# A hybrid encoder step on one core: another order of work inside the attention loop, a lower rate of convolution taps, and fill steps placed elsewhere

## The chip, the cores and the metric

The kernel runs on one core of one Trainium2 chip. A core has five engines that run beside each other, each with its own queue of instructions in order: TensorE (PE in the profile; its weight loads are PEld), VectorE (DVE), ScalarE (ACT), GpSimd (POOL) and SyncE (SP, which here issues DMAs). Matmul results land in PSUM, from which ACT or DVE must copy them out before the buffer can be used again. The metric is the device time of one execution in microseconds (us); less is better.

## What is computed

One layer of a streaming encoder. Its input is 1024 tokens of a new stream and 32 tokens of a running one, each of 1024 channels (1056 tokens in all). What follows is the reference with all that bears on the change:

```
h = rmsnorm(x) ; projections of h: q, k, v, f, ga, ua, ub, gb, ma, mb
q, k = per-head rmsnorm (16 heads of 64) ; c = cumsum(log_sigmoid(f + b_f))
s[t, s'] = q[t].k[s'] + c[t] - c[s']   masked to s' <= t
o = softmax(s) @ v                      # 8 query blocks of 128; block i has (i+1)*128 keys
u = ua * sigmoid(ub)
conv = causal depthwise conv(u), width 31
yb = silu(layernorm(conv) * ln_g + ln_b) * silu(gb) @ w_pb
ya = (o * silu(ga)) @ w_pa
y = x + (sigmoid(ma) * ya + sigmoid(mb) * yb) @ w_out
```

The 32 tokens of the running stream attend to 512 cached keys and to themselves.

## The kernel before

Each of the 1024 columns of a projection group is made in eight weight tiles of 128 columns. Float32 is kept by splitting weights and input into a high and a low half-precision part and adding three products per 128 channels. One weight tile gives three chunks of 352 tokens; one chunk is eight *fill steps* of three matmuls each (`steps`, with `mms` at line 183). After each fill step `beat()` runs: it counts beats and issues whatever is due then, such as parts of the next weight tiles' split (`Batch`: high part on ACT, L138, low part on DVE, L141), and convolution taps, which it hands out at `pace["rate"]` taps a beat.

The convolution runs on DVE: 31 instructions a channel tile (L371), one a tap. When the last channel tile is done, its sum and its sum of squares are added up, and `sides["ready"]` is set; from then on the layernorm's generator (`layernorm`) is advanced by one piece in each step of the attention loop. It first makes the column mean of three chunks with a matmul of ones (L1202), then the variance of three chunks the same way, and then the inverse root in six pieces.

The change is in the attention stage. There PE, SP, DVE and ACT follow the order written in the source (`manual_schedule`); POOL's order is left to the scheduler. `seq` is the list of 132 pieces: 16 heads with eight query blocks each (`Block`, i = 0 to 7), and four pieces of the running stream (`Sample`), each put behind block 0 of heads 3, 7, 11 and 15. The loop takes one piece of `seq` a step and works on several of them at different stages:

- `start`, which is `scores` of piece n+3: the score matmuls on PE into a PSUM tile of tag S (two buffers; L1121, L1122), then on DVE the causal mask added (L1124) and the row maximum (L1126).
- `soft` of piece n+3: the exponential and its row sum on ACT (L1133).
- `norm` of piece n+2: the reciprocal of the row sum on DVE (L1138), and the scaling of the probabilities on POOL (L1139).
- `turn` of piece n, the turning: PE transposes the probabilities in blocks of 128 keys into PSUM tiles of tag T (L1153), up to four blocks in one tile, so blocks i = 4 to 7 need two tiles. The first tile is copied out by ACT, the second by DVE (L1156). POOL zeroes a part of the copy's target (L1146).
- `values` of piece n-2: only at i = 7, for the whole head, 20 products (L1172) into two tiles of tag T, copied and added by ACT (L1176) and DVE (L1177), and multiplied by the gate at odd heads (L1179). At i = 5 of odd heads it only loads that gate. A `Sample` has its own, smaller `values` (L1090).
- `finish` of a `Sample` at piece n-3: one more transpose into tag T (L1099), copied by ACT and DVE.
- `fill(k)`: k fill steps of the 22 gate weight tiles that are kept for this stage (528 fill steps). Their result goes to its own PSUM tiles and is copied out by ACT (L942, L944) and stored by SP.
- the layernorm's piece, whose matmuls (L1202) also use tag T.

Tag T has only two PSUM buffers for all of these: turnings, values, finishes, the layernorm's column sums, and a small sum for each pair of weight tiles (L126).

Of the kernel before, what the change touches and what calls it, by code (L numbers as in the profile page):

```python
# [8 lines left out]
F32 = mybir.dt.float32  # L9
# [5 lines left out]
ALU = mybir.AluOpType  # L15
AX = mybir.AxisListType

D = 1024
T = 1024
# [6 lines left out]
CH = 352  # L26
# [4 lines left out]
LNO = ((0,), (1, 2), (3,), (4, 5), (6,), (7,), ())  # L31
LNEXP = "natural_log_exp_and_others"
NFILL = 22
R_U, R_V, R_QK, R_G, R_A = 0.21, 0.18, 0.165, 0.23, 0.2
NWARM = 34
HT = TT // 2
HC = HT // 2
# [16 lines left out]
def build(tc, xT, xt, wv, wf, ckT, cv, clT, stT, vec, cst, yT, kT, vO, lfO, cpT, csT):  # L54
    nc = tc.nc
# [3 lines left out]
    def pool(name, bufs=1, stack=es, **kw):  # L59
        return stack.enter_context(tc.tile_pool(name=name, bufs=bufs, reuse_waits="tile", **kw))  # L60
# [19 lines left out]
    rstd = lnp.tile([128, TT], F32, name="rstd")  # L80
# [105 lines left out]
    def csl(c):  # L186
        return slice(c * CH, (c + 1) * CH)
# [88 lines left out]
    def t352(name, bufs):  # L276
        return sg.tile([128, CH], F32, name=name, tag=name, bufs=bufs)
# [5 lines left out]
    class Banks:  # L283

        n = 0
# [221 lines left out]
    def newton(out, v, y):  # L507

        nc.vector.tensor_mul(out, y, y)
        nc.vector.scalar_tensor_tensor(out, out, -0.5, v, op0=ALU.mult, op1=ALU.mult)  # L510
        nc.vector.scalar_tensor_tensor(out, out, 1.5, y, op0=ALU.add, op1=ALU.mult)
# [225 lines left out]
    for c in range(4):  # L737
# [16 lines left out]
        for t in range(8):  # L754
            ps = pj.tile([128, 512], F32, name="pjv", tag="pj")
            n = 0
            for kt in range(KT):
                sl = slice(t * 128, t * 128 + 128)
# [243 lines left out]
    psT = pool("psT", 2, stack=p2, space=PS)  # L1002
# [4 lines left out]
    class Two:  # L1007
        n = 0
# [14 lines left out]
    def fill(n):  # L1023
        for _ in range(n):
            next(flow, None)
# [157 lines left out]
    seq = []  # L1183
# [5 lines left out]
    def start(b):  # L1189
        if getattr(b, "i", 1) == 0:  # L1190
            h = b.head
            if h.h % 2 == 0:
                h.ot = heads[h.h + 1].ot = ap.tile([128, T], F32, name="ot", tag="ot", bufs=2)
        b.scores()

    def pending(b):
        return isinstance(b, Sample) or b.i % 2

    def over_channels(acc, put):
        for c in range(3):  # L1200
            pm = psT.tile([128, 512], F32, name="psn", tag="T")
            nc.tensor.matmul(pm[:, :CH], ones_f, acc[:, csl(c)], start=True, stop=True)  # L1202
            put(csl(c), pm[:, :CH])
            yield

    def layernorm():

        shift = sides["shift"]
        for _ in range(4):
            yield  # L1210
        yield from over_channels(mean, lambda sl, ps: nc.scalar.mul(mean[:, sl], ps, 1.0 / D))

        def put(sl, ps):
            t = t352("t", 3)
            nc.scalar.activation(t, mean[:, sl], AF.Square)
            nc.vector.scalar_tensor_tensor(rstd[:, sl], ps, 1.0 / D, t, op0=ALU.mult, op1=ALU.subtract)
            nc.vector.tensor_add(mean[:, sl], mean[:, sl], shift[:, sl])
            nc.vector.tensor_scalar(rstd[:, sl], rstd[:, sl], EPS, None, op0=ALU.add)

        yield from over_channels(rstd, put)  # L1220
        for c in range(6):
            sl = slice(c * CH // 2, c * CH // 2 + CH // 2)
            v, y = rstd[:, sl], t352("t", 3)[:, :CH // 2]
            nc.scalar.activation(y, v, AF.Ln)
            nc.scalar.activation(y, y, AF.Exp, scale=-0.5)
            yield
            w = t352("t", 3)[:, :CH // 2]
            nc.vector.tensor_copy(w, v)
            newton(v, w, y)
            yield  # L1230

    ones_f = cp.tile([128, 128], F32, name="ones_f", tag="ob")
    nc.vector.memset(ones_f, 1.0)
    ln = layernorm()
    sides["shift"] = ap.tile([128, TT], F32, name="shift", bufs=1)
    nc.sync.dma_start(sides["shift"], s_m)
    heads[1].load()
    for n in range(3):
# [3 lines left out]
            seq[n - 1].norm()  # L1242
        fill((8, 4, 0)[n])
    for n, b in enumerate(seq):
        if n + 3 < len(seq):
            start(seq[n + 3])
        if n + 9 < len(seq) and getattr(seq[n + 9], "i", 1) == 0:
            seq[n + 9].head.load()
        if n + 6 < len(seq) and isinstance(seq[n + 6], Sample):
            seq[n + 6].load()  # L1250
        if getattr(b, "i", 0) == 3 and b.head.h + 1 < H:
            heads[b.head.h + 1].load_v()
        b.turn()
        if n + 3 < len(seq):
            seq[n + 3].soft()
        if n + 2 < len(seq):
            seq[n + 2].norm()
        some = 2 if isinstance(b, Sample) or b.i > 2 or b.head.h != 8 else 0
        fill(some)
        if n >= 2 and pending(seq[n - 2]):  # L1260
            seq[n - 2].values()
        fill(some)
        if n >= 3 and isinstance(seq[n - 3], Sample):
            seq[n - 3].finish()
        if "ready" in sides:
            next(ln, None)
# [17 lines left out]
    class Banks3:  # L1284
        n = 0
# [383 lines left out]
```

## Time and profile before

| | |
|---|---|
| median of 3 runs | 1349.14 us (1349.07 to 1354.99) |
| profiled execution, its own time | 1345.89 us |
| its span, first to last instruction | 1344.1 us |
| attention stage | about 566 to 1053 us of the span |
| DVE, ACT, POOL busy over the span | 74%, 53%, 38% |
| mean granted TensorE clock | 0.996 |

In the profile's rows, `out<-in` are the program's names of tiles: `pj` a projection's PSUM tile, `psS` scores, `P` probabilities, `ptr` the transposed ones in PSUM, `pt` their copy, `po` values, `psn` the layernorm's column sums, `ot` a head pair's output, `wh` and `wl` the high and low part of a weight tile. Behind the last bar, or in square brackets, stands the time that the engine was idle just before, and behind the arrow who released it. A group's mean duration of a matmul contains its way through the pipeline, so matmuls that follow each other closely overlap in time.

### The profile page before, as it was taken

How to read it: one execution, taken by the hardware profiler on the slowest of the kernel's cores; microseconds unless marked ns; L12 is line 12 of the kernel's file. 1: busy time of each engine (PE TensorE's matmuls, PEld its weight loads, DVE VectorE, ACT ScalarE, POOL GpSimd, SP SyncE). 2: the span in 40 equal slices, each digit the busy share in tenths (PEclk: the TensorE clock that was granted, in tenths of full speed). 3: DMA queues.
4: the chain of work that ended last, by engine and by line, in shares of the span. 5: the costliest groups of instructions: out<-in, count | busy, mean ns of one | idle time of the engine just before them, and what ended most of it. 6: DMA issues, size and time to landing. Idle time of an engine off the chain costs nothing.

```text
span 1344.1 us, 24837 instructions
## 1 busy us (share of the span) xinstructions
PE 1312.6 (98%) x9383; PEld 1003.1 (75%) x9383; DVE 990.4 (74%) x1532; ACT 719.0 (53%) x1362; POOL 505.8 (38%) x548
## 2 busy tenths in 40 slices
PE   8999999999999999999889998999999999999999
PEld 5687876666666666667567766777776699999998
DVE  6797879888999997987778866655554489166664
ACT  6644555757676743455555555655555566233320
POOL 2001124547484820243433442222222158255562
PEclk8999999999999999999999999999999999999999
DMA  6343233425352463535644643565452698544462
GB/s 251 98 140 104 93 112 118 139 82 187 95 180 87 162 166 109 160 90 155 165 109 123 186 132 99 147 179 132 131 152 54 240 313 262 176 128 146 142 190 69
DMA packets 113496, 194.97 MB, mean 145 GB/s; under 512 B 34080, under 2 KB 80032, under 8 KB 113376
## 3 DMA queue, kind: packets, MB, share of 16 engines
q1 hardware_dynamic: 113232, 193.31, 46.9%
q8 instruction: 74, 1.21, 0.4%
q14 instruction: 46, 0.38, 0.1%
q10 hardware_dynamic: 144, 0.07, 0.0%
HBM read 127.68 MB, written 65.64 MB: 144 GB/s over the span
## 4 chain that ended last, share of the span: by engine, by line
PE 82%; DVE 9%; ACT 3%; issue 2%; DMA 2%; SPq 1%; POOL 0%; DVEq 0%; ACTq 0%; POOLq 0%
PE pj L183 56%; PE pjv L761 6%; PE pj L1501 6%; PE po L1172 4%; PE ptr L1153 3%; DVE nm L1126 2%; DVE wl L141 2%; DVE y L371 2%; PE psS L1122 2%; PE psS L1121 2%; DMA ga<-s_ga 2%; ACT wh L138 1%; DVE psS L1124 1%; DMA s_q<-qh 1%; PE warm L477 1%
## 5 line engine op out<-in xcount | busy, mean ns | idle before, releaser
L183 PE MATMUL pj<-xh,wh 128*128 128x352 f16 (+2 forms) x1536 | 481.6, 314 | 2.3 <-ACT wh L138 1.4
L183 PE MATMUL pj<-xh,wl 128*128 128x352 f16 (+2 forms) x1536 | 481.2, 313 | 0.7 <-DVE wl L141 0.6
L183 PE MATMUL pj<-xl,wh 128*128 128x352 f16 (+2 forms) x1536 | 480.9, 313 | 0.5 <-DVE xl L579 0.4
L183 PEld LDWEIGHTS <-wh 128*128 128x128 f16 x3072 | 301.5, 98 | 162.1 <-issue 7.1
L371 DVE SCALAR_TENSOR_TENSOR y<-u,vec_t,y 128x1086 f32<-128x1086 f32 x240 | 346.8, 1446 | 12.0 <-ACT y L368 8.9
L1139 POOL TENSOR_SCALAR P<-P,nm 128x128 f32<-128x128 f32 (+7 forms) x128 | 129.9, 1015 | 279.9 <-DVE nm L1138 229.8
L183 PEld LDWEIGHTS <-wl 128*128 128x128 f16 x1536 | 150.5, 98 | 72.0 <-DVE wl L141 1.6
L141 DVE SCALAR_TENSOR_TENSOR wl<-raw,sc,wh 128x384 f16<-128x384 f32 (+1 forms) x192 | 128.2, 693 | 48.3 <-ACT wh L138 48.3
L1133 ACT ACTIVATE P<-psS,nm 128x128 f32<-128x128 f32 (+7 forms) x128 | 95.1, 743 | 113.3 <-DVE nm L1138 70.9
L1126 DVE TENSOR_REDUCE nm<-psS 128x1 f32<-128x128 f32 (+7 forms) x128 | 97.0, 758 | 12.5
L1153 PE MATMUL ptr<-ident,P 128*128 128x128 f32 x576 | 88.6, 276 | 17.3 <-DVE pt L1156 9.2
L175 POOL TENSOR_TENSOR wl<-raw,wh 128x384 fp32r<-128x384 f32 (+1 forms) x51 | 63.3, 1270 | 74.3 <-ACT wh L172 58.6
L1153 PEld LDWEIGHTS ptr<-ident,P 128*128 128x128 f32 x576 | 69.2, 141 | 28.2 <-DVE pt L1156 12.1
L1156 ACT COPY pt<-ptr 128x512 f32<-128x512 f32 (+3 forms) x128 | 64.3, 502 | 44.4 <-PE ptr L1153 43.2
L1121 PE MATMUL psS<-KB,QB 128*128 128x256 f32 (+2 forms) x192 | 81.8, 427 | 0.6 <-ACT P L1133 0.6
L880 POOL TENSOR_TENSOR sql<-sqf,sqh 128x352 fp32r<-128x352 f32 x48 | 57.0, 1187 | 65.8 <-ACT sqh L877 65.8
L138 ACT ACTIVATE wh<-raw,sc 128x1024 f16<-128x1024 f32 (+1 forms) x68 | 73.9, 1091 | 8.2 <-DVE sc L158 7.9
L1172 PE MATMUL po<-pt,V 128*64 128x256 f32 x640 | 72.8, 382 | 2.5 <-ACT pts L1078 1.7
L1124 DVE TENSOR_TENSOR psS<-psS,cmask 128x128 f32<-128x128 f32 x128 | 37.6, 294 | 46.0 <-PE psS L1122 45.6
L906 POOL TENSOR_TENSOR ql<-qn,qh 128x352 fp32r<-128x352 f32 (+1 forms) x48 | 67.8, 1429 | 6.6 <-ACT qh L905 6.5
L761 PE MATMUL pjv<-vwh,xh 128*128 128x260 f16 x256 | 70.1, 274 | 0.0
L761 PE MATMUL pjv<-vwl,xh 128*128 128x260 f16 x256 | 70.0, 273 | 0.0
(271 smaller groups left out, 2532.9 us busy)
## 6 DMA issues: line engine op xcount, KB each, us to landing
raw<-wf SPq DMA_DIRECT2D x92, 512.0 KB
QB<-s_q SPq DMA_DIRECT2D x32, 256.0 KB
KB<-s_k SPq DMA_DIRECT2D x32, 256.0 KB
kT<-qn SPq DMA_DIRECT2D x8, 528.0 KB
s_ga<-t SPq DMA_DIRECT2D x24, 176.0 KB
s_gb<-t SPq DMA_DIRECT2D x24, 176.0 KB
s_ma<-t SPq DMA_DIRECT2D x24, 176.0 KB
s_mb<-t SPq DMA_DIRECT2D x24, 176.0 KB
```

The source lines that it names most:

```text
L138: nc.scalar.mul(wh[:, ks, :], raw[:, ks, :], self.s[:, i:i + 1])
L141: nc.vector.scalar_tensor_tensor(wl[:, ks, :], raw[:, ks, :], self.s[:, i:i + 1], wh[:, ks, :], op0=ALU.mult, op1=ALU.subtract)
L183: nc.tensor.matmul(ps, a[:, kt, :], b(kt, sl), start=(first and n == 0), stop=(last and n == N - 1))
L371: t = nc.vector.scalar_tensor_tensor(y, u[:, i:i + CW], w, y, op0=ALU.mult, op1=ALU.add)
L761: nc.tensor.matmul(ps[:, :VC], a, b, start=(n == 0), stop=(n == 23))
L1121: nc.tensor.matmul(ps[:, b, :wm], QB[:, qsl], KB[:, ksl], start=True, stop=False)
L1126: nc.vector.tensor_reduce(nm[:, 0:1], ps[:, :nb, :w], axis=AX.XY, op=ALU.max, negate=True)
L1133: nc.scalar.activation(P[:, :nk].rearrange("p (b w) -> p b w", b=nb), ps[:, :nb, :w], AF.Exp, bias=nm[:, 0:1], accum_out=nm[:, 1:2])
L1139: nc.gpsimd.tensor_scalar(P[:, :nk], P[:, :nk], nm[:, 2:3], 1.0, op0=ALU.mult, op1=ALU.mult)
L1153: nc.tensor.transpose(pt[:, 128 * j:128 * j + 128], P[:, 128 * (4 * u + j):128 * (4 * u + j) + 128], ident)
L1172: nc.tensor.matmul(po[rows], V[:, j, :], parts[c][:, j, :], start=(c % 2 == 0 and j < 2), stop=(c % 2 == 1 and j >= 2 * c))
L1501: nc.tensor.matmul(pss[c][:, :HC], a[:, k, :], x, start=(not more and kt == 0 and n == 0), stop=(kt == 3 and n == 2), skip_group_check=more)
```

## The change

- In a step of the attention loop the turning of piece n and the `norm` of piece n+2 now come ahead of the scores of piece n+3 and of the loads. Before, the order was scores, loads, turning, `soft`, `norm`.
- `values` of piece n-2 come after the loads and before `soft` and the step's fill. Before, they stood between two halves of the fill, with `soft` ahead.
- A step has four fill steps, or three at block 6 of heads 2 to 13. Before, it had two and two, except at blocks 0, 1 and 2 of head 8, which had none.
- The taps' rate in this stage (`R_A`) goes from 0.2 to 0.165 a beat.
- In the layernorm, the square of a chunk's mean is issued one step ahead of the matmul for that chunk's variance. Before, the matmul came first, then the square, and the subtraction that needs both.

```diff
-R_U, R_V, R_QK, R_G, R_A = 0.21, 0.18, 0.165, 0.23, 0.2
+R_U, R_V, R_QK, R_G, R_A = 0.21, 0.18, 0.165, 0.23, 0.165
...
-        def put(sl, ps):
+        for c in range(3):
+            sl = csl(c)
             t = t352("t", 3)
             nc.scalar.activation(t, mean[:, sl], AF.Square)
-            nc.vector.scalar_tensor_tensor(rstd[:, sl], ps, 1.0 / D, t, op0=ALU.mult, op1=ALU.subtract)
+            yield
+            pm = psT.tile([128, 512], F32, name="psn", tag="T")
+            nc.tensor.matmul(pm[:, :CH], ones_f, rstd[:, sl], start=True, stop=True)
+            nc.vector.scalar_tensor_tensor(rstd[:, sl], pm[:, :CH], 1.0 / D, t, op0=ALU.mult, op1=ALU.subtract)
             nc.vector.tensor_add(mean[:, sl], mean[:, sl], shift[:, sl])
             nc.vector.tensor_scalar(rstd[:, sl], rstd[:, sl], EPS, None, op0=ALU.add)
-
-        yield from over_channels(rstd, put)
...
     for n, b in enumerate(seq):
+        b.turn()
+        if n + 2 < len(seq):
+            seq[n + 2].norm()
         if n + 3 < len(seq):
             start(seq[n + 3])
...
         if getattr(b, "i", 0) == 3 and b.head.h + 1 < H:
             heads[b.head.h + 1].load_v()
-        b.turn()
+        if n >= 2 and pending(seq[n - 2]):
+            seq[n - 2].values()
         if n + 3 < len(seq):
             seq[n + 3].soft()
-        if n + 2 < len(seq):
-            seq[n + 2].norm()
-        some = 2 if isinstance(b, Sample) or b.i > 2 or b.head.h != 8 else 0
-        fill(some)
-        if n >= 2 and pending(seq[n - 2]):
-            seq[n - 2].values()
-        fill(some)
+        fill(3 if getattr(b, "i", 0) == 6 and 2 <= b.head.h < 14 else 4)
         if n >= 3 and isinstance(seq[n - 3], Sample):
             seq[n - 3].finish()
```

## Prediction

> **What bounds the kernel now.** I read the page first, then the busy time by stage, then TensorE's waits in the one stage that the diff touches, and last the instructions at its largest gaps. From the page, the span and the engines' busy time.
>
> ```profile
> span 1344.1 us, 24837 instructions
> ...
> PE 1312.6 (98%) x9383; PEld 1003.1 (75%) x9383; DVE 990.4 (74%) x1532; ACT 719.0 (53%) x1362; POOL 505.8 (38%) x548
> ```
>
> TensorE works 98% of the span, and the change adds and removes no matmul, so only its idle time can move: 31.5 us in all. The next view gives busy time in a stretch (stretch, length, then busy us and count of PE, PEld, DVE, ACT, POOL, clock, DMA share, GB/s); 566 to 1053 us is the attention stage.
>
> ```profile
> 566.00:1053.00 487.00, 465.86 (x3460) 336.57 (x3459) 324.17 (x697) 274.85 (x595) 154.54 (x217) 1.00 0.48 130
> ```
>
> The stage holds 487.00 - 465.86 = 21.1 us of TensorE's idle time: the most that any reordering can win, apart from the clock. The waits of TensorE in that stage (who, for whom, us, times, longest):
>
> ```profile
> PE ptr L1153 <- DVE pt L1156: 9.2, 11, 1.7
> PE ptr L1153 <- ACT pt L1156: 6.4, 5, 2.2
> PE po L1172 <- ACT pts L1078: 1.7, 2, 0.9
> ```
>
> So the stall is nearly always the same: a transpose (L1153) or a value product finds both buffers of the PSUM tag T still held, because the copy out (L1156: first four key blocks on ACT, the others on DVE) came late. The copies are short; ACT and DVE are late because bursts of other work stand ahead of them in their written order. The durations, one row a shape (count, busy, mean ns):
>
> ```profile
> L1153 PE MATMUL ptr<-ident,P 128*128 128x128 f32 x576 | 88.6, 276 | 17.3 <-DVE pt L1156 9.2 <-ACT pt L1156 6.4 <-DVE ot L1177 1.2
> L371 DVE SCALAR_TENSOR_TENSOR y<-u,vec_t,y 128x1086 f32<-128x1086 f32 x46 | 64.0, 1391 | 2.3 <-ACT y L368 2.2
> L1156 ACT COPY pt<-ptr 128x512 f32<-128x512 f32 x80 | 46.5, 581 | 21.9 <-PE ptr L1153 21.0
> L1124 DVE TENSOR_TENSOR psS<-psS,cmask 128x128 f32<-128x128 f32 x128 | 37.6, 294 | 46.0 <-PE psS L1122 45.6
> L944 ACT ACTIVATE t<-pj,sc 128x352 f32<-128x352 f32 x66 | 36.1, 546 | 9.4 <-PE pj L183 9.4
> L138 ACT ACTIVATE wh<-raw,sc 128x1024 f16<-128x1024 f32 x22 | 25.1, 1140 | 0.0
> L1133 ACT ACTIVATION_READ_ACCUMULATOR P<-psS,nm 128x1 f32 x128 | 25.0, 195 | 0.0
> L1126 DVE TENSOR_REDUCE nm<-psS 128x1 f32<-128x1024 f32 x16 | 19.6, 1224 | 1.7
> L1133 ACT ACTIVATE P<-psS,nm 128x1024 f32<-128x1024 f32 x16 | 17.9, 1116 | 20.1 <-DVE nm L1126 17.7 <-PE psS L1122 2.4
> ```
>
> **Fills spread.** Before, the first three steps of head 8 have no fill; after, every step has 4, except 3 at block 6 of heads 2 to 13: 12 + 129 x 4 = 528 steps of fill before, 12 + 132 x 4 - 12 = 528 after. What the hole costs (stretches around it, then instructions with their idle time in brackets):
>
> ```profile
> 812.00:836.00 24.00, 19.33 (x111) 12.94 (x110) 13.05 (x29) 10.43 (x22) 4.32 (x9) 0.93 0.51 128
> 824.00:828.00 4.00, 3.43 (x13) 2.62 (x14) 2.51 (x7) 1.81 (x5) 0.80 (x1) 0.69 0.73 197
> 828.00:832.00 4.00, 4.00 (x21) 2.65 (x19) 2.58 (x6) 1.74 (x5) 0.91 (x1) 0.88 0.00 0
> ...
> 816.20 4.54 PE L1172 MATMUL po<-pt,V 128*64 128x256 f32 x40 [0.65 <-ACT mean L1211]
> ...
> 823.48 0.52 PE L1153 MATMUL ptr<-ident,P 128*128 128x128 f32 x3 [1.25 <-DVE ot L1177]
> ...
> 834.27 0.33 PE L1153 MATMUL ptr<-ident,P 128*128 128x128 f32 x1 [2.20 <-ACT pt L1156]
> ```
>
> 24.00 - 19.33 = 4.67 us idle, and the granted clock falls to 0.69 and 0.88 for two stretches of 4 us: (0.31 + 0.12) x 4 = 1.7 us of slower matmuls. The layernorm's six column sums, which take the same PSUM buffers, fall into the same hole; the 2.20 us is theirs, behind a weight's high part on ACT. After, they come some fourteen steps later, with fill around them: I leave 0.7 us of idle and count -4.0 and -1.7. The fill taken from block 6 costs nothing while the copies of that step are out: 12 matmuls of fill last 1.79 us (row below), so 0.45 us of cover goes, ahead of a turning whose scores were the narrowest; if a burst stands there it costs that 0.45, 12 times 5.4 at the very most.
>
> [...]
>
> **Tap rate 0.2 to 0.165.** A conv tap (L371, 1.39 us on DVE) comes every 5 beats before, every 6 after; the work is the same, 46 taps and 4 sums, spread over (50 / 0.2 - 12) / 4 = 60 steps before and (50 / 0.165 - 12) / 4 = 73 after. DVE's largest pile-up with ACT, where the last channel's start, its square, a weight's high part and a fill's copy meet:
>
> ```profile
> 639.00:651.00 12.00, 8.26 (x53) 5.61 (x52) 9.56 (x15) 7.94 (x13) 6.25 (x4) 1.00 0.67 190
> ...
> 640.69 1.28 ACT L368 ACTIVATE y<-u,vec_t 128x1086 f32<-128x1086 f32 x1
> ...
> 643.98 0.33 PE L1153 MATMUL ptr<-ident,P 128*128 128x128 f32 x1 [1.14 <-ACT pt L1156]
> ```
>
> That stretch idles 12.00 - 8.26 = 3.74 us. The channel's start lies in the fill of step 18, beat 12 + 18 x 4 + 2 = 86; it moves to about 86 x 0.2 / 0.165 = 104, some five steps on, and the weights do not move, so the two part; it then lands just ahead of the first running-stream block, so I count only -2.3. The other late copies (21.1 - 4.67 - 3.74 - 3.83 in the next paragraph = 8.9 us) happen mostly while taps run; with 0.165 / 0.2 = 0.83 of the taps in a step, -1.3. Bounds: 0 and -3.
>
> **Turnings before scores, reciprocals sooner.** No instruction is added. On DVE the copy of block n now stands ahead of the mask and maximum of block n+3, which at 1024 keys are 0.29 + 1.22 = 1.52 us sooner out; but the scores that lay between a fill and the next turning are gone from there too. Both orders put one fill and one set of scores between two turnings. In exchange the scores, and so the maximum and the exponential, come later by a turning (88.6 / 576 = 0.154 us a transpose, 1.2 us at eight) and by DVE's copy and reciprocal, which are short. ACT has the next copy behind that exponential. After the scores of block 7 ended: 0.29 + 1.22 + 1.12 + 0.20 and handovers of some 0.3 = 3.1 us, then the copy of block 5, 0.58: 3.7. TensorE meanwhile fills 1.79, turns block 5 in 0.9, scores a narrow block (0.4) and fills again: 4.9. That leaves 1.2 us, 0.6 with a fill's copy (0.55) ahead, none with a weight's high part (1.14). Before, the same copy had 1.6 us. So DVE's side gains and ACT's loses by like amounts: 0, between -4 (half of the 9.2 that waits for DVE) and +13 (rival 1). The moved queue work: the pt zeroing on POOL and the running block's value load on SP go ahead of the scores' loads, the gate load ahead of the fill's stores; all are needed a step later or more, 0. The reciprocal asks for an exponential that is one fill older; if it is late DVE waits in front of a mask whose scores are not there yet, 0.
>
> **Values before the whole fill, finish before the turning.** Covers that go:
>
> ```profile
> 663.90 1.30 PE L1172 MATMUL po<-pt,V 128*64 128x256 f32 x10 [0.94 <-ACT pts L1078]
> ...
> 785.18 1.08 PE L1172 MATMUL po<-pt,V 128*64 128x256 f32 x8 [0.79 <-ACT pts L1078]
> ...
> 681.37 0.33 PE L1153 MATMUL ptr<-ident,P 128*128 128x128 f32 x1 [1.05 <-ACT pt L1156]
> ...
> 1038.39 0.33 PE L1153 MATMUL ptr<-ident,P 128*128 128x128 f32 x1 [1.04 <-ACT pt L1156]
> ...
> 609.43 1.79 PE pj L183 x12
> ```
>
> Values of a head stand behind a running block's turning four times, with half a fill (0.9 us) between before and one set of scores (about 0.5) after: 0.94 + 0.79 of stalls grow by 0.4 at each of four. A running block's finish was followed by scores, now by a wide turning straight: 1.05 + 1.04 grow by about 0.2 at each of four, as the copies wait for ACT either way. With these 3.83 us go to 6.0: +2.2. At ordinary heads the turning before takes one buffer, and the two copies of the values are out under 1.79 us of fill: 0. The exponential now waits on ACT behind the values' copies, but 1.79 us of fill and a turning follow: 0, up to 0.5 a head if not.
>
> **Square a step ahead.** Three squares leave the way between product and evacuation; it wins at most the 0.7 that I left in the layernorm, and costs the same 0.7 where a column sum stands straight in front of a wide turning. 0.
>
> **Sum.** -4.0 - 1.7 - 2.3 - 1.3 + 2.2 = -7.1 us. The profiled execution took 1345.89 us (span 1344.1), 3.25 below the median of the three runs, 1349.14; so 1338.8 for a profile and 1342.0 for the median.
>
> **The rivals.** (1) Slower: the exponential that comes a turning later holds up ACT's copies. Place: the turnings of blocks 5 and 6, 32 in all, with 1.2 us to spare or 0.6. It decides from (7.1 + 6.7) / 32 = 0.43 us of wait at each; at 0.6 it is +19 - 7.1 = +12, 1361 us. For it: ACT's exponentials of 1024 keys already waited 17.7 us for the maximum. Against: ACT is busy 275 of 487 us. Price if each loses 0.4: +12.8 - 7.1, 1355.
> (2) No change: the hole closes (-5.7), but the stalls of the bursts only move, and the lost covers and the waits of rival 1 in a mild form eat the rest: -7.1 + 2.3 + 1.3 + 2 = -1.5, 1347.6. For it: the idle time hangs on bursts whose work is unchanged.
> (3) Much faster: DVE's copy ahead of the maximum ends the 9.2 us that waits for DVE too: -7.1 - 7.9 = -15, 1334.
> (4) The clock does not follow the hole, and the 1.7 us come back elsewhere: 1343.7. The trace speaks against it, as the fall stands right at the idle times of the hole.
>
> **How the numbers follow.** A time 0.5% from the median, 6.7 us, is about what a measurement of this kernel can tell from no change. My forecast has 0.40, (3) 0.15, (2) 0.17, (4) 0.06, (1) 0.22. The forecast lies just past that bound, so 0.08 of its 0.40 count with no change, as do (2), (4) and 0.02 of (1) in a mild form: faster 0.32 + 0.15 = 0.47, same 0.08 + 0.17 + 0.06 + 0.02 = 0.33, slower 0.20. The range 1332 to 1355 leaves out (1) beyond its price of 0.4 a turning and what is past (3).
>
> **What would show it.** Right: no stretch of the attention stage under a granted clock of 0.9, no idle over 1 us in head 8, waits of transposes for DVE under 7 us, and 13 to 15 us of idle in the stage. Wrong: waits of transposes for ACT's copy well over 6.4 us, at blocks 5 and 6 (rival 1), or products of values waiting for L1156 or L1078 by more than 4 us; or the clock falling again somewhere.

## The result, and the profile after

The changed kernel takes 1368.57 us (median, 1367.05 to 1370.12), the kernel before 1351.52 us on the same chip: a ratio of 1.0126 with an interval of 1.01 to 1.0153. It is 1.3% slower; the forecast was 0.5% faster. The profiled execution took 1368.43 us, its span 1366.6 us, 22.5 us more than before.

The page of the changed kernel, then its busy time in the attention stage (stretch, length, busy us and count of PE, PEld, DVE, ACT, POOL, clock, DMA share, GB/s):

```profile
span 1366.6 us, 24779 instructions
...
PE 1320.9 (97%) x9383; PEld 994.3 (73%) x9383; DVE 992.1 (73%) x1532; ACT 714.3 (52%) x1362; POOL 476.7 (35%) x548
```

```profile
566.00:1075.00 509.00, 475.22 (x3466) 328.40 (x3464) 327.31 (x699) 269.98 (x594) 124.34 (x217) 0.99 0.46 125
```

TensorE idles 509.00 - 475.22 = 33.8 us in the stage, where it idled 21.1 before: +12.7. The stage itself, from the first score to the last product of values, went from 486.8 to 507.8 us, so nearly all of the 22.5 us lie in it. Who TensorE waited for in the stage (for whom, us, times, longest):

```profile
PE ptr L1153 <- ACT pt L1156: 15.8, 17, 2.4
PE po L1172 <- ACT pts L1078: 6.9, 4, 2.3
PE ptr L1153 <- DVE os_t L1102: 2.6, 2, 1.8
PE ptr L1153 <- ACT mean L1211: 2.3, 2, 1.3
PE ptr L1153 <- DVE pt L1156: 1.3, 2, 1.1
PE po L1172 <- ACT pt L1156: 1.2, 1, 1.2
```

The change did to DVE's copies what it says: the waits for them fell from 9.2 to 1.3 us. The waits for ACT's copies (L1156 and L1078) rose from 6.4 + 1.7 to 15.8 + 6.9 + 1.2 us. The reason stands in what ACT itself waits for, in the same view of ACT, first of the kernel before and then of the kernel after:

```profile
ACT P L1133 <- DVE nm L1138: 70.9, 62, 3.1
ACT pt L1156 <- PE ptr L1153: 43.2, 50, 2.1
ACT P L1133 <- DVE nm L1126: 38.4, 30, 3.3
```

```profile
ACT P L1133 <- DVE nm L1126: 125.0, 79, 4.0
...
ACT pt L1156 <- PE ptr L1153: 11.7, 17, 2.0
...
ACT P L1133 <- DVE nm L1138: 2.1, 2, 1.7
```

The lines of L1133 are exponentials. Those that the view puts down to the reciprocal (L1138) waited for a maximum too: before, these 62 start 0.09 to 0.40 us, mostly 0.095, behind the end of their own block's maximum, and the short reciprocal (0.15 us on the mean) is only what DVE finished last. So ACT waits for maxima in both kernels: from the records of all 128 exponentials, it idles 113.3 us in front of them before and 152.6 after. The larger change is where in the order this idle time falls. Before, ACT was often ready for the copy and waited 43.2 us for the transposes; that is the good case, as the copy then starts at once, 0.04 us behind them. After, this wait is only 11.7 us: when ACT comes to a copy, the transposes have mostly been done for some time. From the records of all 128 turnings, the mean time from the end of a first tile's transposes to the start of its copy went from 0.55 to 1.15 us, and 83 copies are over 0.5 us late instead of 42. Added up, the copies are 147.0 us late instead of 69.9; ACT is idle in front of an exponential for 27.1 us of that (10.7 before), runs one for 57.4 (25.4 before), and does other work queued ahead of the copy for most of the rest. One such turning, block 5 of head 0 (start, duration, engine, instruction, idle time before it; other rows left out):

```profile
587.53 1.23 DVE L1126 TENSOR_REDUCE nm<-psS 128x1 f32<-128x1024 f32 x1
588.74 0.82 PE L1153 MATMUL ptr<-ident,P 128*128 128x128 f32 x6
588.87 1.11 ACT L1133 ACTIVATE P<-psS,nm 128x1024 f32<-128x1024 f32 x1 [2.45 <-DVE nm L1126]
589.98 1.14 ACT L138 ACTIVATE wh<-raw,sc 128x1024 f16<-128x1024 f32 x1
591.02 0.54 ACT L944 ACTIVATE t<-pj,sc 128x352 f32<-128x352 f32 x1
591.45 0.58 ACT L1156 COPY pt<-ptr 128x512 f32<-128x512 f32 x1
592.18 0.63 PE L1153 MATMUL ptr<-ident,P 128*128 128x128 f32 x4 [0.57 <-ACT pt L1156]
```

ACT idles 2.45 us for the maximum of block 7. Behind the exponential stand a weight's high part and a fill's copy; the weight's part could have run in that idle time, as it does at 586.28 in a run shown below. Then comes the copy, 1.9 us after the transposes ended (589.56), and the next turning waits. Both pieces run between the transposes and the copy in 13 of the 83 late cases, a fill's copy in 54. In this trace nothing on ACT overtook the exponential in those 2.45 us.

Where the idle time fell, by the turning it stands in front of: the second tile of block 4 went from 5.4 to 9.7 us, value products from 2.4 to 8.1, all tiles of blocks 5 and 6 from 6.6 to 8.4. Block 4's growth is that of the four turnings that follow a running piece's `finish`: they waited 1.05, 0.00, 0.10 and 1.04 us before, and 1.99, 1.76, 0.86 and 2.43 after. Two of these running-stream places:

```profile
665.32 7.08 PE L1172 MATMUL po<-pt,V 128*64 128x256 f32 x40 [2.27 <-ACT pts L1078]
...
683.42 1.01 ACT L1133 ACTIVATE P<-psS,nm 128x896 f32<-128x896 f32 x1 [1.78 <-DVE nm L1126]
684.41 1.14 ACT L138 ACTIVATE wh<-raw,sc 128x1024 f16<-128x1024 f32 x1
685.45 0.19 ACT L1101 COPY os_t<-ptr 64x64 f32<-64x64 f32 x1
685.55 0.58 ACT L1156 COPY pt<-ptr 128x512 f32<-128x512 f32 x1
686.18 0.33 PE L1153 MATMUL ptr<-ident,P 128*128 128x128 f32 x1 [1.99 <-ACT pt L1156]
```

The 40 matmul records at 665.32, of one head's 20 products, last 7.08 us where 40 such records lasted 4.54 at 816.20 in the kernel before. The granted clock is at half from 663.68, within their wait, to 670.51. It fell at three of these places (the same columns as in the stage's row):

```profile
664.00:668.00 4.00, 2.68 (x14) 1.54 (x16) 2.64 (x4) 1.41 (x4) 3.07 (x6) 0.50 1.03 224
668.00:672.00 4.00, 4.00 (x28) 2.35 (x26) 0.68 (x1) 0.58 (x1) 0.41 (x2) 0.69 1.00 238
684.00:692.00 8.00, 6.01 (x30) 3.88 (x29) 5.29 (x11) 4.37 (x9) 1.01 (x1) 0.79 0.03 12
1056.00:1064.00 8.00, 5.71 (x27) 3.70 (x28) 3.92 (x9) 3.93 (x10) 1.01 (x1) 0.79 0.06 23
```

That is (0.50 + 0.31) x 4 + 0.21 x 8 + 0.21 x 8 = 6.6 us of clock. Some 0.7 us of it, half of the 1.32 us from 664 to 665.32, falls on a wait in which TensorE idled anyway, which leaves 5.9 us of slower matmuls against 1.7 before: +4.2. With the idle time, 12.7 + 4.2 = 16.9 of the 22.5 us. Some 4 of the rest lie in the stage without showing as idle time (the last section says how that can be), and 1.5 outside it.

These figures are of two executions. By the medians the loss is 1368.57 - 1351.52 = 17.1 us; the profiled execution of the kernel before, 1345.89 us, is one of its faster ones. The clock's share varies too: the mean granted clock is 0.990 to 0.995 in the four executions of the changed kernel, and 0.991 to 0.996 in those of the kernel before that stand beside the experiments.

### The profile page after: what moved, and what is told of

Same layout as the page of the kernel before. It is cut to its first block, busy times and chain, and to the rows that moved or that the text cites. A ratio compares the mean times of both kernels' runs of the same rounds, so it can differ in the third digit from the quotient of the medians.

```text
span 1366.6 us, 24779 instructions
## 1 busy us (share of the span) xinstructions
PE 1320.9 (97%) x9383; PEld 994.3 (73%) x9383; DVE 992.1 (73%) x1532; ACT 714.3 (52%) x1362; POOL 476.7 (35%) x548
## 3 DMA queue, kind: packets, MB, share of 16 engines
q8 instruction: 74, 1.21, 0.4%
## 4 chain that ended last, share of the span: by engine, by line
PE 76%; DVE 9%; ACT 5%; DMA 5%; issue 3%; SPq 1%; POOL 1%; ACTq 0%; DVEq 0%; POOLq 0%
PE pj L183 53%; PE pjv L761 6%; PE pj L1501 5%; PE po L1172 3%; DMA ga<-s_ga 3%; PE ptr L1153 3%; DVE nm L1126 3%; PE psS L1122 2%; PE psS L1121 1%; DVE y L371 1%; DVE wl L141 1%; ACT P L1133 1%; ACT wh L138 1%; DVE psS L1124 1%; DMA s_y<-y 1%
## 5 line engine op out<-in xcount | busy, mean ns | idle before, releaser
L183 PEld LDWEIGHTS <-wh 128*128 128x128 f16 x3072 | 301.9, 98 | 180.5 <-issue 22.7
L1139 POOL TENSOR_SCALAR P<-P,nm 128x128 f32<-128x128 f32 (+7 forms) x128 | 95.8, 748 | 292.8 <-DVE nm L1138 281.8
L1133 ACT ACTIVATE P<-psS,nm 128x128 f32<-128x128 f32 (+7 forms) x128 | 95.0, 742 | 152.6 <-DVE nm L1126 125.0
L1153 PE MATMUL ptr<-ident,P 128*128 128x128 f32 x576 | 90.3, 277 | 24.4 <-ACT pt L1156 15.8
L1172 PE MATMUL po<-pt,V 128*64 128x256 f32 x640 | 75.9, 392 | 8.2 <-ACT pts L1078 6.9
L1121 PE MATMUL psS<-KB,QB 128*128 128x256 f32 (+2 forms) x192 | 76.4, 399 | 0.0
L1172 PEld LDWEIGHTS po<-pt,V 128*64 128x64 f32 x640 | 45.2, 140 | 35.8 <-ACT pts L1078 8.6
L1156 ACT COPY pt<-ptr 128x512 f32<-128x512 f32 (+3 forms) x128 | 64.1, 501 | 11.9 <-PE ptr L1153 11.7
```

The costliest lines, as they stand in the source:

```text
L183: nc.tensor.matmul(ps, a[:, kt, :], b(kt, sl), start=(first and n == 0), stop=(last and n == N - 1))
L1121: nc.tensor.matmul(ps[:, b, :wm], QB[:, qsl], KB[:, ksl], start=True, stop=False)
L1133: nc.scalar.activation(P[:, :nk].rearrange("p (b w) -> p b w", b=nb), ps[:, :nb, :w], AF.Exp, bias=nm[:, 0:1], accum_out=nm[:, 1:2])
L1139: nc.gpsimd.tensor_scalar(P[:, :nk], P[:, :nk], nm[:, 2:3], 1.0, op0=ALU.mult, op1=ALU.mult)
L1153: nc.tensor.transpose(pt[:, 128 * j:128 * j + 128], P[:, 128 * (4 * u + j):128 * (4 * u + j) + 128], ident)
L1172: nc.tensor.matmul(po[rows], V[:, j, :], parts[c][:, j, :], start=(c % 2 == 0 and j < 2), stop=(c % 2 == 1 and j >= 2 * c))
```

## The experiments

Each ratio is to the kernel before on the same chip, with its interval. All kernels compute the whole reference. "Late" stands for the mean time from a turning's transposes to its copy on ACT, in the profiled execution, as above.

### The parts of the change, one by one

Fills spread alone, on the kernel before:

```diff
-        some = 2 if isinstance(b, Sample) or b.i > 2 or b.head.h != 8 else 0
-        fill(some)
+        fill(2)
...
-        fill(some)
+        fill(1 if getattr(b, "i", 0) == 6 and 2 <= b.head.h < 14 else 2)
```

> The kernel before with only the fill steps spread (2 + 2 in every step, 2 + 1 at block 6 of heads 2 to 13). By my prediction's step on the fills: -4.0 us of idle and -1.7 us of clock, ratio to before 0.996, no fall of the granted clock in head 8. By the theory that the hole was only where other stalls met: ratio 0.999 to 1.001, the idle time at other steps.

Measured: 1348.52 us, 0.9989 (0.9972 to 1.0007): nothing that can be told from no change. Of the 4.67 us of idle time in head 8, two waits of 1.62 and 1.54 us are left, at blocks 4 and 5, where the prediction left 0.7 in all. The whole stage idles 23.3 us instead of 21.1, and the clock falls elsewhere: its row around 780 us has a granted clock of 0.79.

```profile
776.00:784.00 8.00, 5.75 (x28) 3.67 (x29) 7.37 (x18) 3.80 (x9) 1.43 (x2) 0.79 0.36 119
```

The taps' rate alone, on the kernel before:

```diff
-R_U, R_V, R_QK, R_G, R_A = 0.21, 0.18, 0.165, 0.23, 0.2
+R_U, R_V, R_QK, R_G, R_A = 0.21, 0.18, 0.165, 0.23, 0.165
```

> The kernel before with only the tap rate 0.2 -> 0.165. By my prediction's step: -2.3 - 1.3 us, ratio 0.997; the 3.74 us of idle around the last channel's start gone. If the rate is what made the changed kernel slower (the pile-up moved onto a running-stream block): above 1.002, with idle time near that block.

Measured: 1345.6 us, 0.9959 (0.9945 to 0.9974): some 5.5 us won. Its profile does not show how. The stage idles 20.95 us instead of 21.1: around the last channel's start one wait of 1.86 us is left (647.7 us), and waits of 2.29 and 1.40 us are new elsewhere (887.5 and 922.5 us). The profiled execution, 1346.51 us at a mean granted clock of 0.995, is not faster than that of the kernel before (1345.89 us at 0.996).

All of the change but the loop's new order (fills spread, rate, square a step ahead):

```diff
     for n, b in enumerate(seq):
-        b.turn()
-        if n + 2 < len(seq):
-            seq[n + 2].norm()
         if n + 3 < len(seq):
...
+        b.turn()
-        if n >= 2 and pending(seq[n - 2]):
-            seq[n - 2].values()
         if n + 3 < len(seq):
             seq[n + 3].soft()
-        fill(3 if getattr(b, "i", 0) == 6 and 2 <= b.head.h < 14 else 4)
+        if n + 2 < len(seq):
+            seq[n + 2].norm()
+        fill(2)
+        if n >= 2 and pending(seq[n - 2]):
+            seq[n - 2].values()
+        fill(1 if getattr(b, "i", 0) == 6 and 2 <= b.head.h < 14 else 2)
```

> The changed kernel with the loop's old order: fills spread, tap rate 0.165 and the square a step ahead, but scores, turning, exponential, reciprocal, half fill, values, half fill as before. If the order alone made the change slower: ratio to before 0.991 to 0.997 (the sum of my steps on fills and taps, -9 us at best). If the rate or the square takes part in the loss: above 1.000.

Measured: 1340.5 us, 0.9922 (0.9901 to 0.9943), late 0.49 us.

The loop's new order alone, on the kernel before (the first three blocks of head 8 without fill, as before):

```diff
     for n, b in enumerate(seq):
+        b.turn()
+        if n + 2 < len(seq):
+            seq[n + 2].norm()
         if n + 3 < len(seq):
...
-        b.turn()
+        if n >= 2 and pending(seq[n - 2]):
+            seq[n - 2].values()
         if n + 3 < len(seq):
             seq[n + 3].soft()
-        if n + 2 < len(seq):
-            seq[n + 2].norm()
-        some = 2 if isinstance(b, Sample) or b.i > 2 or b.head.h != 8 else 0
-        fill(some)
-        if n >= 2 and pending(seq[n - 2]):
-            seq[n - 2].values()
-        fill(some)
+        fill(4 if isinstance(b, Sample) or b.i > 2 or b.head.h != 8 else 0)
```

> The kernel before with only the loop's new order (turning and reciprocal ahead of the scores, values ahead of the whole fill); tap rate 0.2, hole in head 8 and square as before. If the order alone made the change slower, it is slower than the changed kernel, since it lacks the gains of the fills and taps: ratio to before 1.015 to 1.025, the added time in the steps of the running-stream blocks and in the wide turnings behind their finish. If the parts only do harm together: below 1.008.

Measured: 1372.58 us, 1.0165 (1.014 to 1.0189), late 1.08 us. The order alone makes the kernel slower; the rest of the change makes it faster.

### The covers

From here on the edits stand on the changed kernel. Half of the fill back in front of the values that follow a running piece:

```diff
+        if isinstance(b, Sample):
+            fill(2)
         if n >= 2 and pending(seq[n - 2]):
             seq[n - 2].values()
...
-        fill(3 if getattr(b, "i", 0) == 6 and 2 <= b.head.h < 14 else 4)
+        fill(3 if getattr(b, "i", 0) == 6 and 2 <= b.head.h < 14 else 2 if isinstance(b, Sample) else 4)
```

> The changed kernel with two of the four fill steps of a running-stream block's step put between its turning and the values of the head before it; all else as changed. Theory A (most of the loss is lost cover at the four running-stream blocks: their steps grew by 8.6 us and the block-4 steps behind their finish by 7.7): -6 to -9 us against the changed kernel, values' waits for the running block's copies from 6.9 to under 2 us. Theory B (the exponential a turning later makes ACT's copies late at every wide turning): -2 us at most.

Measured: 1362.14 us, 1.0094 (1.008 to 1.0108). By the ratios some 4.3 us come back, between the two theories; the values' waits for the running block's copies fell from 6.9 to 3.3 us, not under 2.

The running piece's `finish` between two halves of the fill instead of behind it:

```diff
+        first = 2 if n >= 3 and isinstance(seq[n - 3], Sample) else 0
+        fill(first)
-        fill(3 if getattr(b, "i", 0) == 6 and 2 <= b.head.h < 14 else 4)
         if n >= 3 and isinstance(seq[n - 3], Sample):
             seq[n - 3].finish()
+        fill((3 if getattr(b, "i", 0) == 6 and 2 <= b.head.h < 14 else 4) - first)
```

> The changed kernel with a running block's finish between the halves of the fill instead of behind the whole fill, straight in front of a wide turning. Theory A: -6 to -9 us against the changed kernel, block-4 steps of heads 3, 7, 11 and 15 down from 4.4 to 7.4 us each to about 3.5. Theory B: -2 us at most.

Measured: 1367.97 us, 1.0136 (1.0122 to 1.015): no gain. Both together:

> Both covers in the changed kernel. Theory A: -13 to -18 us against the changed kernel, near or below the kernel before (ratio 0.995 to 1.003), and the granted clock without falls at the running blocks. Theory B: -4 us at most, ratio to before still above 1.008.

Measured: 1360.94 us, 1.0085 (1.0071 to 1.0099), late 1.21 us. The covers are worth 1.0126 - 1.0085 = 0.0041, some 5.5 us, most of it at the values (0.0032 with their cover alone). That is far from theory A's 13 to 18 us and just past theory B's 4. The finish's cover fails because its copies, on ACT and DVE, are as late as the others:

```profile
PE ptr L1153 <- ACT pt L1156: 12.4, 15, 1.6
PE ptr L1153 <- DVE os_t L1102: 6.7, 4, 2.3
```

These are TensorE's waits in the kernel with both covers: what stood behind `finish` is still there (1.76, 1.76, 0.91 and 2.31 us), with half a fill in between.

### Which part of the order

Both covers, and the scores ahead of the turning again:

```diff
     for n, b in enumerate(seq):
+        if n + 3 < len(seq):
+            start(seq[n + 3])
         b.turn()
         if n + 2 < len(seq):
             seq[n + 2].norm()
-        if n + 3 < len(seq):
-            start(seq[n + 3])
```

> Both covers, and the scores ahead of the turning again (values still ahead of the rest of the fill). Against the run with both covers it tells what the turning in front of the scores costs by itself. Theory B: -8 us or more, and ACT's waits for the row maximum, 125.0 us in the changed kernel and 38.4 before, back under 60. Theory A: within 3 us of the run with both covers, whatever those waits do.

Measured: 1341.13 us, 0.9939 (0.9925 to 0.9952), late 0.50 us. On the same chip as the run with both covers, these lines alone are worth 1360.94 - 1341.13 = 19.8 us. The same waits in this kernel:

```profile
PE ptr L1153 <- DVE pt L1156: 8.7, 8, 1.9
PE ptr L1153 <- ACT pt L1156: 2.3, 4, 0.7
PE ptr L1153 <- DVE os_t L1102: 1.9, 4, 0.9
```

TensorE's waits for ACT's copies fall from 12.4 to 2.3 us, the stalls behind `finish` fall to 0.39, 0.39, 0.19 and 0.95, and DVE's copies are late again (8.7). The expectation's 38.4 and 125.0 us leave out the waits under the reciprocal's name; counted whole, ACT idles 89.6 us in front of exponentials here, 152.5 with both covers and 113.3 in the kernel before.

Next, the place of the reciprocals, with both covers. Behind the scores in the new order (turning, scores, `norm`):

> The run with both covers (1360.9 us, 1.0085), only the reciprocal of block n+2 put behind the scores' mask and maximum again; the turning still in front. Theory B1 (the turning in front delays the exponential and with it ACT's copies): within 4 us of that run, ratio to before 1.005 to 1.010. Theory B2 (the early reciprocal makes DVE wait for an exponential, 22.7 us of waits that the kernel before had at 0.2, and holds up mask and maximum): 12 us or more faster, ratio below 1.000.

Measured: 1358.5 us, 1.0062 (1.0042 to 1.0083), late 1.02 us. Ahead of all in the old one (`norm`, scores, turning):

> The run with both covers and scores ahead of the turning (1341.1 us, 0.9939), with only the reciprocal put ahead of the mask and maximum. B1: within 4 us of it, ratio 0.993 to 0.997. B2: 12 us or more slower, above 1.002.

Measured: 1344.2 us, 0.9962 (0.9949 to 0.9975). Sooner reciprocals cost 0.0023 in either order, some 3 us; the intervals overlap, so this is a hint. The turning ahead of the scores then costs 1.0062 - 0.9939 or 1.0085 - 0.9962, 0.0123 either way, some 16.6 of the 19.8 us. In the profile after, DVE waits 22.7 us for ACT's row sum in front of them, and the masks and maxima stand behind.

The two orders taken apart; for this, the mask and maximum of `scores` become `maxima`, and the copies of `turn` become `copies`. PE turns first, but DVE has mask and maximum ahead of its copy:

```diff
         b.turn()
-        if n + 2 < len(seq):
-            seq[n + 2].norm()
         if n + 3 < len(seq):
             start(seq[n + 3])
+        if n + 3 < len(seq):
+            seq[n + 3].maxima()
+        b.copies()
+        if n + 2 < len(seq):
+            seq[n + 2].norm()
```

> Both covers; TensorE turns block n ahead of the scores as in the change, but on DVE mask and maximum stand ahead of the copy and the reciprocal, as in the kernel before. If the loss comes from DVE's order (copy and reciprocal ahead of the maximum): ratio 0.993 to 0.998. If it comes from the scores lying a turning later on TensorE: 1.005 to 1.012.

Measured: 1369.26 us, 1.0148 (1.0124 to 1.0173), late 0.89 us: slower than either forecast. Here the late mask and maximum hold up DVE's own copies as well, which start 1.85 us behind their transposes instead of 0.71 with both covers. TensorE's waits (here L1165 is the transpose, L1172 the copy, L1149 the reciprocal):

```profile
PE ptr L1165 <- DVE nm L1149: 13.0, 13, 2.0
...
PE ptr L1165 <- ACT pt L1172: 5.1, 7, 1.2
```

Each of the 13 waits under the reciprocal's name ends 0.15 us after a copy on DVE ended, so they are waits for DVE's copies.

PE scores first, but DVE copies ahead of mask and maximum:

```diff
     for n, b in enumerate(seq):
+        if n + 3 < len(seq):
+            start(seq[n + 3])
         b.turn()
+        b.copies()
         if n + 2 < len(seq):
             seq[n + 2].norm()
         if n + 3 < len(seq):
-            start(seq[n + 3])
+            seq[n + 3].maxima()
```

> Both covers; TensorE makes the scores ahead of the turning as in the kernel before, but DVE does the copy and the reciprocal ahead of mask and maximum, as in the change. If the loss comes from DVE's order: 1.005 to 1.012. If it comes from TensorE's order: 0.993 to 0.998.

Measured: 1352.24 us, 1.0022 (1.0008 to 1.0035), late 0.92 us: between the two forecasts. With the scores first, DVE's copy and reciprocal ahead of the maximum cost 1.0022 - 0.9939 = 0.0083 (the reciprocal alone 0.0023), though DVE's own copies come sooner (0.67 us behind their transposes instead of 0.94). So either engine's order makes a loss: whatever brings the maximum later, a turning on PE or a copy on DVE, makes ACT's copies later (0.89 to 1.21 us in these runs, 0.50 with the scores first), and where the late maximum also stands ahead of DVE's copy, that copy is late too.

### The exponential behind the copy

If the loss is the exponential ahead of the next copy in ACT's queue, moving that instruction behind the copy should end it, and the turnings can stay in front. With both covers:

```diff
         start(seq[n])
-        seq[n].soft()
+        if n < 2:
+            seq[n].soft()
...
         b.turn()
         if n + 2 < len(seq):
-            seq[n + 2].norm()
+            seq[n + 2].soft()
         if n + 3 < len(seq):
             start(seq[n + 3])
+        if n + 2 < len(seq):
+            seq[n + 2].norm()
...
-        if n + 3 < len(seq):
-            seq[n + 3].soft()
```

> Both covers and the turning ahead of the scores, but the exponential of a block is issued on ACT one step later, behind the next turning's copy, and the reciprocal behind the mask and maximum. Beside the run with the reciprocal behind (1358.5 us, 1.0062) only the exponential's place differs. If the loss is that ACT's copy stands in ACT's queue behind an exponential whose scores were made only a fill earlier: 8 us or more faster than that run, ratio 0.993 to 1.000, and the mean delay of the copy behind its turning, 1.02 us there and 0.55 in the kernel before, under 0.6. If the loss is elsewhere (the scores' own lateness, a later product or scaling): ratio above 1.004.

Measured: 1330.02 us, 0.9844 (0.9825 to 0.9864), late 0.10 us: more than was expected, and faster than both kernels. Its stage, TensorE's waits and ACT's waits:

```profile
566.00:1036.00 470.00, 463.37 (x3459) 326.15 (x3459) 330.52 (x698) 273.73 (x594) 159.48 (x217) 1.00 0.50 135
```

```profile
PE ptr L1153 <- ACT pt L1156: 2.0, 3, 0.7
PE ptr L1153 <- DVE pt L1156: 1.3, 2, 1.1
PE ptr L1153 <- POOL P L1139: 1.3, 4, 0.8
PE ptr L1153 <- DVE os_t L1102: 1.2, 2, 1.0
PE po L1172 <- ACT pts L1078: 0.5, 1, 0.5
```

```profile
ACT pt L1156 <- PE ptr L1153: 86.1, 81, 2.9
...
ACT P L1133 <- DVE nm L1138: 4.6, 6, 2.0
...
ACT P L1133 <- DVE nm L1126: 0.5, 1, 0.5
```

TensorE idles 470.00 - 463.37 = 6.6 us, the clock is 1.00, and ACT's two waits have changed places: 5.1 us for maxima (the 4.6 under the reciprocal's name included), 86.1 us for transposes. Beside the run with the reciprocal behind (1.0062), the exponential's place is worth 1.0062 - 0.9844 = 0.0218, some 29 us. The turning shown above, in this kernel:

```profile
586.28 1.15 ACT L138 ACTIVATE wh<-raw,sc 128x1024 f16<-128x1024 f32 x1
...
588.35 0.82 PE L1153 MATMUL ptr<-ident,P 128*128 128x128 f32 x6
588.55 0.56 ACT L944 ACTIVATE t<-pj,sc 128x352 f32<-128x352 f32 x1 [1.12 <-PE pj L183]
589.01 0.57 ACT L1156 COPY pt<-ptr 128x512 f32<-128x512 f32 x1
589.47 1.13 ACT L1133 ACTIVATE P<-psS,nm 128x1024 f32<-128x1024 f32 x1
591.06 0.60 PE L1153 MATMUL ptr<-ident,P 128*128 128x128 f32 x4
```

The same exponential starts 1.12 us behind the start of the turning instead of 0.13, with its maximum long there, and nobody waits for it.

Two more ask what that order owes to its parts. Without the covers:

> The kernel after, with nothing changed but the place of the exponential: soft of piece n+2 (not n+3) comes behind the turning of piece n, and norm of that piece behind the scores of n+3. No cover is put back. If the exponential ahead of ACT's copy is the whole of the loss, the covers are worth as much as with the order of the kernel after (ratio 1.0085 against 1.0126, some 5.5 us): about 1335.5 us, ratio 0.9885, and the delay of ACT's copy behind its turning at 0.10 to 0.15 us as in the run that has both. If the covers hide only waits that the late copies cause, they are worth nothing now: 1330, ratio 0.984. If they matter on their own, ratio above 0.992.

Measured: 1332.05 us, 0.9871 (0.9856 to 0.9886), late 0.10 us: between the two cases, with the first case's 0.9885 in its interval and the second's 0.984 outside. The covers may still be worth some 0.0027, but the intervals overlap. With the covers, and the scores ahead of the turning and the exponential:

> The run with both covers and the later exponential, with the scores of piece n+3 ahead of the turning of piece n and of the exponential of n+2, as the kernel before has them. It asks which order is the better one once the exponential isn't ahead of ACT's copy. If my theory is complete, ACT's copies are out as early in either order, but DVE's copy stands behind a mask and a maximum again, as in the kernel before (mean delay 1.10 us against 0.55): some 32 wide turnings with DVE copies of blocks 6 and 7 lose up to 0.2 us each, so ratio 0.988 to 0.991 (1335 to 1339), slower than turning first with 0.9844. Rival: the turning in front of the scores is of no use in itself, then 0.982 to 0.986.

Measured: 1331.68 us, 0.986 (0.9843 to 0.9876), late 0.07 us. TensorE's waits:

```profile
PE ptr L1153 <- DVE pt L1156: 4.7, 6, 1.5
PE ptr L1153 <- ACT pt L1156: 2.0, 3, 0.7
```

The waits for DVE are there as expected, but small, and the time is not to be told from 0.9844. Turning first is no measurable gain of its own even where it does no harm: the rival holds, and what counts is the exponential's place.

### Two side questions

A still lower rate, 0.14, with the old order (against 0.9922 with 0.165):

> The run with the old order (fills spread, rate 0.165, square ahead; 0.9922) with the tap rate at 0.14. If a slower pace of taps is itself the gain: 0.987 to 0.991. If 0.165 won by where a pile-up fell: 0.992 to 0.997.

Measured: 1344.78 us, 0.9949 (0.9931 to 0.9967). A slower rate does not go on to win, so the gain of 0.165 is likelier where its bursts fall than the fewer taps in a step; the intervals overlap a little.

Both copies of a turning on ACT, with the old order:

```diff
-                (nc.vector.tensor_copy if u else nc.scalar.copy)(p[:, 4 * u:4 * u + nj, qo], p3)
+                nc.scalar.copy(p[:, 4 * u:4 * u + nj, qo], p3)
```

> The run with the old order (0.9922) with the second copy of a wide turning on ACT too instead of DVE. Its transposes still wait 10.4 us for DVE's copy and 3.3 for ACT's. If DVE's queue alone makes those waits: -4 to -8 us, ratio 0.986 to 0.990. If ACT's copies then queue behind the exponential as in the changed kernel: 0.993 or above.

Measured: 1334.91 us, 0.9876 (0.9856 to 0.9896). The transposes' 10.4 us of waits for DVE's copy are gone, and those for ACT's are 4.8 us instead of 3.3. So in the old order DVE's queue, with masks and maxima ahead of the second copy, held most of the remaining waits.

## Why the prediction was wrong

**What bounds the kernel** held: TensorE's idle time in the stage is what moves, by way of the two buffers of tag T, and the best order leaves 6.6 of the 21.1 us.

**Turnings before scores, reciprocals sooner: 0** is the step that failed. Measured, the two together cost 19.8 us, some 16.6 the turnings and perhaps 3 the reciprocals. Its statement that DVE's side gains and ACT's loses by like amounts was half right: DVE's waits fell by 7.9 us, as rival 3 had hoped, but ACT's rose by twice that, and the clock's falls cost 5.9 us instead of 1.7. The working compared one copy's end with the next turning, 3.7 us against 4.9, on an ACT queue with one extra piece in it. In the turning shown two pieces (a weight's high part and a fill's copy) stand behind the waiting exponential at once; the weight's part was kept from running by the wait itself. And it looked only at ordinary turnings, while four times the copy is wanted by a running piece's extra use of tag T.

**Rival 1** (the exponential that comes a turning later holds up ACT's copies) had the mechanism, and its sign in the profile came: 15.8 us of waits against 6.4. So did the other two signs of being wrong, the values' waits over 4 us and the falls of the clock. Its place was wrong: not 0.4 us at each of 32 turnings of blocks 5 and 6, whose idle time grew by 1.7 us in all, but 1 to 2 us at a few places around the running pieces, with the clock after them. The argument against it, that ACT is busy 275 of 487 us, was none: ACT was idle and blocked at once. With 0.22 for it against 0.40 the chances were not far off, but the range ended at 1355 because it left out rival 1 past 0.4 us a turning; the same rival at 0.6, 1361, was nearer.

**Values before the whole fill, finish before the turning: +2.2** had the sign right. The stalls that it puts from 3.83 to 6.0 us went to 6.9 + 7.0 = 13.9. Putting the covers back wins 5.5 us, all at the values; the `finish` stalls follow from the turnings' order (1.76 with the cover, 0.39 with the scores first), which this term did not count. (Its working has two slips that change little: the four stalls make 3.82 us, and 0.4 and 0.2 at four places each make 2.4, not 2.2.)

**Fills spread: -4.0 and -1.7** is not shown. Head 8 kept 3.2 us of its idle time, other waits grew (23.3 us idle in the stage), the clock fell elsewhere (0.79 at 780 us), and the time stayed the same within what was measured. This is what rivals 2 and 4 said of the stalls and of the clock.

**Tap rate: -2.3 - 1.3 = -3.6** held as a number: -5.5 us with an interval from -3.5 to -7.4. Its mechanism is not shown, since idle time of the stage stayed at 20.95 us in the profiled execution, so that the number fits is partly luck. Its second half, fewer taps in a step, is not borne out by the run at 0.14.

**Square a step ahead: 0** was not tried by itself. It is in the run without the new order, whose 0.9922 is 0.0026 below the sum of the two parts measured alone; whether the square or the parts together make that stays open.

**The clock.** The prediction put the fall in head 8 down to the hole, and so took its 1.7 us as won with it. There the half rate starts at 825.51 us, 2.0 us behind a wait of 1.25 us. In the changed kernel the three falls came within or just behind waits of 2.27, 1.99 and 2.43 us around a running piece (half rate from 663.68, 687.58 and 1059.63 us; the waits end at 665.32, 686.18 and 1058.29 us). Such a wait is not enough by itself: one of 2.29 us that ended at 920.93 us brought no fall. What decides was not shown.

## What to carry to other kernels

On ACT, where nothing overtook an exponential that waited 2.45 us, a wait cost what stood behind it. So an instruction that waits for a long chain (scores, mask, maximum, exponential) belongs behind the short copies that free the PSUM buffers TensorE needs next: here the exponential's place was worth some 29 us (ratios of 1.0062 and 0.9844). Low busy time is no sign that an engine has room (ACT was busy 270 of 509 us while its first copies came 147.0 us late in sum); read its own waits, and ask of each wait in front of an instruction what is queued behind it. When the order of one engine's work is changed, look at the rare steps that use the scarce buffers once more than the others (here four of 132) before multiplying a small price by the many ordinary ones.

## What was not expected of the hardware

The idle time of TensorE shows less than the waits cost. Twelve fill matmuls start 1.79 us / 12 = 0.149 us apart when nothing holds them, but each is listed with some 0.31 us, so the listed times of neighbours overlap. By these two figures I estimate that a wait of up to about 0.16 us hides in the listed duration. By this reading the 4 us of the stage's loss that neither the idle time nor the clock explains are many short waits; that was not tested by itself. Two runs with the same order on TensorE fit it, both covers without and with the later exponential: their stages last 501.6 and 469.9 us, and idle time, (502.00 - 470.69) - (470.00 - 463.37), makes 24.7 us of the difference of 31.7. Of the other 7.0 us, 2.9 stand in the busy time listed for the same 576 transposes, 89.9 against 87.0 us; the granted clock is 1.00 in both stages.

The clock's falls in this stage were alike in length: in the record of the granted clock the half rate lasts 3.41 us in the kernel before (from 825.51 us) and twice in the kernel after (from 687.58 and 1059.63 us), and 6.83 us from 663.68 us on. I estimate from these that a fall of 3.41 us in which TensorE has work throughout costs half of it, 1.7 us of matmul time; the long one cost (6.83 - 1.64) / 2 = 2.6, as TensorE idled for its first 1.64 us. The length of the wait ahead of it did not show in that: waits of 1.25, 1.99 and 2.43 us all had falls of 3.41 us behind them.
